# A decoder layer on Trainium2: keys, queries and two value blocks of its memory attention as paired products

## The chip, the cores and the metric

The kernel runs on one core of one Trainium2 chip. The metric is the device time of one execution in microseconds. Before the change it is 1982.21 us, the median of three runs (1981.88 to 1982.49). One execution was also recorded with a hardware profiler; that execution took 1980.76 us, and its span from first to last instruction is 1979.0 us.

A core has five engines, each with its own queue of instructions that it works through in the order of the program: TensorE does matrix products (PE in the profile, and PEld for its loads of the stationary operand), VectorE (DVE) and ScalarE (ACT) do elementwise work, GpSimd (POOL) does a few small operations here, and SyncE (SP) issues the DMA transfers.

## The reference, cut to what matters

One layer with four stages, of which the third is the one that changes. `x` is 256 tokens by 2048, `mem` is 256 memory tokens by 2048, and there are 4 heads of 512.

```python
def rmsnorm(x, w):
    y = x * lax.rsqrt(jnp.mean(x * x, axis=-1, keepdims=True) + 1e-6)
    return y * w

def memory_cross_attention(hn, mem_n, w_q, w_k, w_v, w_o):
    q = (hn @ w_q).reshape(b, s, 4, 512)
    k = (mem_n @ w_k).reshape(b, m, 4, 512)
    v = (mem_n @ w_v).reshape(b, m, 4, 512)
    logits = jnp.einsum("bshd,bmhd->bhsm", q, k) * 512 ** -0.5
    p = jax.nn.softmax(logits, axis=-1)
    o = jnp.einsum("bhsm,bmhd->bshd", p, v).reshape(b, s, 2048)
    return o @ w_o

def layer(x, mem, ...):
    ...                                     # retention and RG-LRU mixers, gated merge
    h = x + merged @ w_mix_out
    h = h + memory_cross_attention(rmsnorm(h, norm_xa_w), rmsnorm(mem, norm_mem_w), ...)
    h = h + conv_gated_ffn(rmsnorm(h, norm_ffn_w), ...)
    return rmsnorm(h, final_norm_w)
```

All of it is float32.

## The kernel before, in words

**Products.** A float32 product is made of three products of float32r parts. Every operand is split into a rounded part `hi` and a rest `lo`, and hi*hi, lo*hi and hi*lo are added up in PSUM (`products_n`, lines 404 to 411). One product of a 128x128 stationary block with a 128x512 moving block is thus three matmuls. All matmuls are kept in the order in which the program text asks for them.

**Weights.** The weights lie in one DRAM array in the order of use, and are loaded by SP in chunks of 1 MB into three buffers `raw`. `prefetch` (line 273) keeps the split parts of the next chunks ready (`AHEAD = 2`): `weight_parts` (line 344) makes `hi` with a cast on ACT (line 349) and `lo` with a subtraction on DVE (line 350), each into one of six buffers (`PART_BUFS = 6`). A buffer comes free when the matmuls of the chunk that lies in it are done. Each chunk is one step of a counter; `later(n, fn)` (line 377) runs `fn` some steps on.

**Single products.** `gemm_n`/`steps_n` (line 413) makes one block of 512 output columns for 256 tokens in four steps of 24 matmuls. Its left side is a list of eight split tiles, each for two of the sixteen 128-row blocks of the contraction. Where that list is made on demand (class `Pairs`, line 661: `xs` for x, `ms` for the memory tokens), the single product asks for tiles ahead of their use, in line 434: `st[min(NT, k0 + 3 * n) // 2 - 1]`.

**Pairs.** `pair`/`steps_pair` (line 475) makes two blocks of 512 columns at once in eight steps. An ordinary step has 24 matmuls. In the steps named by a tuple (`SEVEN = (2, 5)` and others) the 2x2 blocks of tokens and columns are multiplied with seven products in place of eight, so 21 matmuls. Such a step needs sums of weight blocks (`seven_parts`, line 364: four additions on DVE, line 370, and 3.5 casts and subtractions of 128x1024) and sums of token blocks (`sums_of`, line 442: a sum of the parts, three differences, a rounding on ACT in line 458 and a rest on DVE in line 459). A pair uses all eight PSUM banks: three tiles of `acc` and the two tiles of `sm` (`small`, line 209). After its last step the banks are added up into two row tiles `o` (lines 511 to 530). The lines on the left side of a pair are

```python
for i in seven:
    if k2 < i <= k2 + 3 and (not isinstance(st, list) or i < len(st)):
        sums_of(st[i])
t = st[k2]
```

so sums are made up to three steps ahead for tiles that exist, and `st[k2]`, asked for in the step that uses it, makes the tile if it does not exist yet.

**Turning.** `by_dma` (line 544) turns rows into columns: ACT copies the rows into planes of 16-bit halves (line 552), SP issues two transposing DMAs, and some steps later ACT joins the halves (line 565).

**Memory attention.** The residual rows `hrow` (four tiles of 256 tokens by 512 columns) get the product with `w_mix_out` added (`residual`, line 1008; the addition is line 1023) and are turned into `h1s`, eight split tiles. Meanwhile `memory_steps` (line 1045) makes the row norms of the memory tokens and the first four of the eight tiles of `ms`. Then, for each of the four heads, `key_query` makes the keys (`xa_w_k` with `ms`) and the queries (`xa_w_q` with `h1s`) as single products; `softmax` (line 1065) follows a few steps later, with the logits in one of the two `sm` tiles. Four single products for the values follow, each with `attend` (line 1109), and then the output product with `xa_w_o`, whose first two blocks are already a pair. `hrow` stays in SBUF all the time. The pool `big` has 29 buffers of 4 KB per partition, and nearly everything named here lies in it.

Of the kernel before, what the change touches and what calls it, by code (L numbers as in the profile page):

```python
# [9 lines left out]
F32 = mybir.dt.float32  # L10
# [7 lines left out]
P = 128  # L18
D = 2048
S = 256  # L20
NT = D // P
# [3 lines left out]
XH = 4  # L25
XD = D // XH
FF = 5632
# [47 lines left out]
def weight_plan():  # L75
# [12 lines left out]
    plan += [("w_mix_out", 0, NT, b * BW) for b in range(4)]  # L88
    plan += [(w, 0, NT, b * BW) for b in range(4) for w in ("xa_w_k", "xa_w_q")]
    plan += [("xa_w_v", 0, NT, b * BW) for b in range(4)]  # L90
    plan += [both("xa_w_o", 0, SEVEN_O)] + [("xa_w_o", 0, NT, b * BW) for b in (2, 3)]
# [74 lines left out]
def hybrid_layer(  # L166
# [23 lines left out]
    sp_ = ctx.enter_context(tc.tile_pool(name="sp", bufs=2))  # L190
    pm = ctx.enter_context(tc.tile_pool(name="pm", bufs=3, space=bass.MemoryType.PSUM))
    px = ctx.enter_context(tc.tile_pool(name="px", bufs=2, space=bass.MemoryType.PSUM))

# [243 lines left out]
    def gemm_n(*args):  # L437
        return ended(steps_n(*args))
# [35 lines left out]

    def steps_pair(w, row, st, nk, c1, c2, seven=SEVEN):

        last = max(seven)
        banks, begun = {}, set()
# [53 lines left out]
    def pair(*args):  # L532
        return ended(steps_pair(*args))
# [279 lines left out]
    for g in range(2):  # L813
# [18 lines left out]
        if g == 1:  # L832
            vs += [split_rows(v, rs0) for v in pair("w_in", 0, xs, NT, O_V + 1024, O_V + 1024 + BW, SEVEN_V)]
        qr, kr = turned
# [173 lines left out]
    def residual(w, st, out, wcol, steps=None):  # L1008

        ss = sums()  # L1010
        products = [steps_n(w, 0, st, NT, b * BW) for b in range(4)]
        sources = []
        for b in range(4):
            if steps:
                steps(b)
                if b == 0:
                    for one in products[:3]:
                        for _ in range(2):
                            next(one)
            elif b == 0:  # L1020
                sources += pair(w, 0, st, NT, 0, BW, SEVEN_O)
            h = hrow[b]
            dve.tensor_add(h, h, sources.pop(0) if sources else ended(products[b]))
            by_dma(h, lambda f, b=b: turn(f, b, out, wcol), 1 + (b == 1), b == 3 and steps is None)
            if b < 2:
                later(2 + b, lambda h=h, b=b: squares(h, ss, b))
            else:
                squares(h, ss, b)
        return ss
# [25 lines left out]

    h1s = []
    ss1 = residual("w_mix_out", merged, h1s, p_xa, memory_steps)


    lscale = sp_.tile([P, 2], F32, tag="ls", name="lscale")  # L1060
# [29 lines left out]
    def split_block(f, out, seven=()):  # L1090
        for pr in range(2):
            with_sums(out, seven, f[:, 2 * pr : 2 * pr + 2, :])
        return out

    def key_query(b):
        ks = []
        turned_rows(gemm_n("xa_w_k", 0, ms, NT, b * BW), rsms[0], lambda f: split_block(f, ks))

        def query(f):
            qs = split_block(f, [])  # L1100
            later(1, lambda: softmax(b, qs, ks))

        turned_rows(gemm_n("xa_w_q", 0, h1s, NT, b * BW), None, query)

    for b in range(XH):
        key_query(b)
    osp = []
# [13 lines left out]

    for b in range(XH):
        v = split_rows(gemm_n("xa_w_v", 0, ms, NT, b * BW), rsms[0])
        later(1, lambda b=b, v=v: attend(b, v))

    h2s = []
# [113 lines left out]
    def up(b, hid, seven):  # L1240
# [6 lines left out]

        two = pair("ffn_w_up", 0, h2s, NT, b * BW, FF + b * BW, SEVEN_U)
        for a, then, wait in zip(two, (lambda f: conv(f, 4 * b, gt), value), (1, 3)):
# [61 lines left out]
```

## Time and profile before

| | before |
|---|---|
| median of 3 runs | 1982.21 us |
| the profiled execution: its time | 1980.76 us |
| the profiled execution: its span | 1979.0 us |
| TensorE matmul, share of the span | 99% |
| VectorE, ScalarE, share of the span | 79%, 69% |
| DMA, mean rate | 215 GB/s |

How to read the profile lines below: the page has a line of busy times for each engine, and a chain of waits that is followed back from the last instruction. A group line reads `line engine operation output<-inputs shapes xcount | busy us, mean ns of one | idle time before, and what ended it`. A timeline line reads `start us, us, engine line operation xcount [idle before <-what ended it]`. A line of a view of stretches has, for each engine, its busy time and the number of its instructions, then the granted TensorE clock, the share of the DMA engines and their rate. A line of waits has the engine and tile that waited, for whom, us in total, how often, and the longest.

### The profile page before, as it was taken

The numbers are of one execution on the slowest core, as the hardware profiler recorded it, in microseconds if no ns is written. First come the engines' busy times: TensorE is split into PE (matmuls) and PEld (weight loads), VectorE is DVE, ScalarE is ACT, GpSimd is POOL, SyncE is SP. The second block draws the span as 40 slices with busy tenths as digits, with TensorE's granted clock in tenths as the row PEclk, the third lists the DMA queues.
The fourth block names the chain that finished last, engine by engine and source line by source line (L and its number), as shares of the span: only waits on it lengthen the run. The fifth ranks groups of instructions, "written<-read, shape, count | busy, mean of one in ns | idle before, by whom it ended". The sixth has DMA issues, their size and how long they took to land.

```text
span 1979.0 us, 24013 instructions
## 1 busy us (share of the span) xinstructions
PE 1965.8 (99%) x8834; PEld 1631.4 (82%) x8834; DVE 1564.5 (79%) x2050; ACT 1367.1 (69%) x1671; POOL 26.8 (1%) x25
## 2 busy tenths in 40 slices
PE   9999999999999999999999999999999999999998
PEld 7888788888888888888888888888888888888887
DVE  6887986899898888767555567778889878898686
ACT  7666657989654656697676667777776578774683
POOL 0000010010000000000000000000000000000000
PEclk9999999999999999999999999999999999999999
DMA  9755567666555465887676657666666566666673
GB/s 334 238 213 173 194 232 203 213 210 212 194 212 189 176 228 192 297 277 226 218 222 206 203 170 223 210 216 213 224 207 208 212 211 215 215 210 233 214 252 110
DMA packets 197190, 425.62 MB, mean 215 GB/s; under 512 B 142032, under 2 KB 146640, under 8 KB 152016
## 3 DMA queue, kind: packets, MB, share of 16 engines
q1 hardware_dynamic: 197072, 424.09, 64.2%
q8 instruction: 69, 1.13, 0.2%
q14 instruction: 49, 0.40, 0.1%
HBM read 388.39 MB, written 2.10 MB: 197 GB/s over the span
## 4 chain that ended last, share of the span: by engine, by line
PE 91%; DVE 3%; ACT 3%; issue 1%; DMA 1%; SPq 0%; POOL 0%; POOLq 0%; DVEq 0%; ACTq 0%
PE acc L251 66%; PE sm L251 25%; DVE lo L350 1%; DMA raw<-in_wall 1%; ACT hi L349 1%; ACT f L565 1%; ACT pl L552 0%; DMA pt<-pl 0%; DVE xr L932 0%; DVE tb L734 0%; ACT rows L804 0%; DMA raw<-in_head 0%; DVE fv L1138 0%; DVE o L530 0%; DVE raw L370 0%
## 5 line engine op out<-in xcount | busy, mean ns | idle before, releaser
L251 PE MATMUL acc<-hi,s 128*128 128x512 f32 (+1 forms) x3976 | 1218.7, 388 | 0.2 <-ACT s L611 0.2
L350 DVE TENSOR_TENSOR lo<-raw,hi 128x1024 fp32r<-128x1024 f32 (+1 forms) x794 | 931.8, 1197 | 325.7 <-ACT hi L349 315.8
L349 ACT CAST hi<-raw 128x1024 fp32r<-128x1024 f32 (+1 forms) x794 | 788.3, 1023 | 401.1 <-PE acc L251 126.6
L251 PEld LDWEIGHTS acc<-hi,s 128*128 128x128 f32 x3976 | 743.4, 188 | 152.4 <-ACT s L611 0.5
L251 PE MATMUL acc<-lo,s 128*128 128x512 f32 (+1 forms) x1988 | 771.0, 388 | 1.4 <-DVE lo L350 1.4
L251 PEld LDWEIGHTS acc<-lo,s 128*128 128x128 f32 x1988 | 373.3, 188 | 79.8 <-DVE lo L350 3.1
L251 PE MATMUL sm<-hi,s 128*128 128x512 f32 x1344 | 414.0, 389 | 1.6 <-DVE o L530 1.6
L251 PEld LDWEIGHTS sm<-hi,s 128*128 128x128 f32 x1344 | 252.1, 188 | 55.0 <-ACT v L600 1.8
L251 PE MATMUL sm<-lo,s 128*128 128x512 f32 x672 | 261.5, 389 | 0.0
L565 ACT COPY f<-pt 128x1024 uint16<-128x1024 uint16 x128 | 167.1, 1353 | 36.2 <-DMA pt<-pl 35.8
L251 PEld LDWEIGHTS sm<-lo,s 128*128 128x128 f32 x672 | 126.2, 188 | 26.1
L370 DVE TENSOR_TENSOR raw<-raw 128x512 f32<-128x512 f32 x160 | 110.0, 687 | 2.4
L251 PE MATMUL acc<-hi,ts 128*128 128x512 f32 x240 | 73.9, 389 | 0.0
L552 ACT COPY pl<-rows 128x1024 uint16<-128x1024 uint16 x56 | 55.7, 1042 | 24.8 <-DVE rows L576 13.3
L552 ACT COPY pl<-o 128x1024 uint16<-128x1024 uint16 x52 | 51.6, 1038 | 6.7 <-DVE o L1000 6.7
L251 PEld LDWEIGHTS acc<-hi,ts 128*128 128x128 f32 x240 | 45.0, 188 | 9.3
L251 PE MATMUL acc<-lo,ts 128*128 128x512 f32 x120 | 47.1, 393 | 1.4 <-DVE lo L350 1.3
L1138 DVE SCALAR_TENSOR_TENSOR fv<-f,pf,fv 128x255 f32<-128x255 f32 (+1 forms) x88 | 38.3, 476 | 0.0
L530 DVE TENSOR_TENSOR o<-o,acc 128x512 f32<-128x512 f32 x52 | 33.2, 678 | 5.7 <-PE acc L251 5.7
L1138 DVE SCALAR_TENSOR_TENSOR fg<-f,pf,fg 128x255 f32<-128x255 f32 (+1 forms) x88 | 35.8, 477 | 0.0
L520 DVE TENSOR_TENSOR o<-o,acc 128x512 f32<-128x512 f32 x52 | 35.2, 678 | 0.0
L530 DVE TENSOR_TENSOR o<-o,sm 128x512 f32<-128x512 f32 x52 | 33.9, 677 | 0.1
(190 smaller groups left out, 1010.8 us busy)
## 6 DMA issues: line engine op xcount, KB each, us to landing
raw<-in_wall SPq DMA_DIRECT2D x352, 1024.0 KB, 4.9
nat<-in_x SPq DMA_DIRECT2D x8, 512.0 KB, 9.2
raw<-in_wall SPq DMA_DIRECT2D x7, 512.0 KB, 6.2
pt<-pl SPq DMA_TRANSPOSE x128, 3.3
nat<-in_mem SPq DMA_DIRECT2D x4, 512.0 KB, 8.9
xt<-in_x_t SPq DMA_DIRECT2D x3, 512.0 KB, 9.3
xt<-in_mem_t SPq DMA_DIRECT2D x3, 512.0 KB, 6.4
dec<-in_consts SPq DMA_DIRECT2D x2, 512.0 KB, 4.4
```

The lines of the kernel that those rows point to most:

```text
L251: tc.keep_in_program_order(pe.matmul(*a, **k))
L349: act.copy(hi[:, cs], src[:, cs])
L350: dve.tensor_tensor(out=lo[:, cs], in0=src[:, cs], in1=hi[:, cs].bitcast(F32), op=ALU.subtract)
L370: dve.tensor_tensor(out=o, in0=a, in1=b, op=ALU.add)
L520: dve.tensor_tensor(out=o, in0=a, in1=b, op=op)
L530: dve.tensor_tensor(out=o, in0=o, in1=banks[a], op=ALU.add)
L552: act.copy(planes[:, tt], words[:, tt])
L565: act.copy(halves_[:, :, :, cs], turned_[:, :, :, cs])
L1138: dve.scalar_tensor_tensor(out=y[:, s:S], in0=z[:, j, 0 : S - s], scalar=pf[:, 2 - s, t : t + 1], in1=y[:, s:S], op0=ALU.mult, op1=ALU.add,)
```

## The change

Keys, queries and the first two value blocks become pairs with seven products in steps 2 and 5: keys of heads 0 and 1, queries of 0 and 1, queries of 2 and 3, then the softmax of heads 0 and 1, keys of 2 and 3, values of 0 and 1, the softmax of heads 2 and 3, and the values of 2 and 3 as single products as before. The key rows are scaled in place on ACT and turned directly, where before DVE scaled or copied each block's rows out of PSUM. The stored token sums are dropped after the first pair of keys, and made again for the second. The four residual tiles are stored to DRAM when they are complete, and loaded again before the output product. A pair takes its tuple of seven-product steps from the plan of the weights rather than from its caller, with the same values as before for the old pairs.

```diff
--- before.py
+++ after.py
@@ -86,8 +86,8 @@
     plan += [both("w_in", O_GB + 1024), both("w_proj_rnn", 1024)]
     plan += [both(w, c + b * BW) for w, c in (("w_in", O_GA), ("w_proj_ret", 0)) for b in (0, 2)]
     plan += [("w_mix_out", 0, NT, b * BW) for b in range(4)]
-    plan += [(w, 0, NT, b * BW) for b in range(4) for w in ("xa_w_k", "xa_w_q")]
-    plan += [("xa_w_v", 0, NT, b * BW) for b in range(4)]
+    plan += [both(w, b * BW) for w, b in (("xa_w_k", 0), ("xa_w_q", 0), ("xa_w_q", 2), ("xa_w_k", 2))]
+    plan += [both("xa_w_v", 0)] + [("xa_w_v", 0, NT, b * BW) for b in (2, 3)]
     plan += [both("xa_w_o", 0, SEVEN_O)] + [("xa_w_o", 0, NT, b * BW) for b in (2, 3)]
     for kind, *a in ff_plan():
         if kind == "down" and sum(a) < NF // 4:
@@ -189,6 +189,7 @@
     tp = ctx.enter_context(tc.tile_pool(name="tp", bufs=10))
     sp_ = ctx.enter_context(tc.tile_pool(name="sp", bufs=2))
     pm = ctx.enter_context(tc.tile_pool(name="pm", bufs=3, space=bass.MemoryType.PSUM))
+    home = ctx.enter_context(tc.tile_pool(name="home", bufs=4, space=bass.MemoryType.DRAM))
     px = ctx.enter_context(tc.tile_pool(name="px", bufs=2, space=bass.MemoryType.PSUM))
 
     count = [0]
@@ -472,8 +473,9 @@
             sums_of(t, src, scale)
         out.append(t)
 
-    def steps_pair(w, row, st, nk, c1, c2, seven=SEVEN):
-
+    def steps_pair(w, row, st, nk, c1, c2):
+
+        seven = plan[gemms[0]][3][2]
         last = max(seven)
         banks, begun = {}, set()
         banks["p2"], banks["p4"] = (lambda a: (a[:, 0, :], a[:, 1, :]))(acc())
@@ -830,7 +832,7 @@
                 v = gemm_n("w_in", 0, xs, NT, O_V + b * BW) if b else ended(v_steps)
                 vs.append(split_rows(v, rs0))
         if g == 1:
-            vs += [split_rows(v, rs0) for v in pair("w_in", 0, xs, NT, O_V + 1024, O_V + 1024 + BW, SEVEN_V)]
+            vs += [split_rows(v, rs0) for v in pair("w_in", 0, xs, NT, O_V + 1024, O_V + 1024 + BW)]
         qr, kr = turned
         gates = []
         c = O_G + g * 1024
@@ -1018,7 +1020,7 @@
                         for _ in range(2):
                             next(one)
             elif b == 0:
-                sources += pair(w, 0, st, NT, 0, BW, SEVEN_O)
+                sources += pair(w, 0, st, NT, 0, BW)
             h = hrow[b]
             dve.tensor_add(h, h, sources.pop(0) if sources else ended(products[b]))
             by_dma(h, lambda f, b=b: turn(f, b, out, wcol), 1 + (b == 1), b == 3 and steps is None)
@@ -1053,9 +1055,18 @@
             for k2 in range(4):
                 later(2 + k2, lambda k2=k2: ms[k2])
 
-    h1s = []
+    h1s, parked = [], []
+
+    def park(h):
+        t = home.tile([P, 2, BW], F32, tag="home", name=nm("home"))
+        sp.dma_start(out=t, in_=h)
+        parked.append(t)
+
     ss1 = residual("w_mix_out", merged, h1s, p_xa, memory_steps)
 
+
+    for h in hrow:
+        park(h)
 
     lscale = sp_.tile([P, 2], F32, tag="ls", name="lscale")
     dve.tensor_scalar_mul(lscale, rstd_rows(ss1), float(XD**-0.5))
@@ -1092,18 +1103,22 @@
             with_sums(out, seven, f[:, 2 * pr : 2 * pr + 2, :])
         return out
 
-    def key_query(b):
-        ks = []
-        turned_rows(gemm_n("xa_w_k", 0, ms, NT, b * BW), rsms[0], lambda f: split_block(f, ks))
-
-        def query(f):
-            qs = split_block(f, [])
-            later(1, lambda: softmax(b, qs, ks))
-
-        turned_rows(gemm_n("xa_w_q", 0, h1s, NT, b * BW), None, query)
-
-    for b in range(XH):
-        key_query(b)
+    keys, queries = {}, {}
+
+    def turned_pair(w, st, b, r, out):
+
+        for i, a in enumerate(pair(w, 0, st, NT, b * BW, (b + 1) * BW)):
+            if r is not None:
+                with tc.high_priority(FREE):
+                    for tt in range(2):
+                        act.mul(a[:, tt, :], a[:, tt, :], r[:, tt : tt + 1])
+            o = out[b + i] = []
+            by_dma(a, lambda f, o=o: split_block(f, o), 1 + i)
+
+    def attention(b):
+        for i in (b, b + 1):
+            softmax(i, queries[i], keys[i])
+
     osp = []
 
     def attend(b, v):
@@ -1119,9 +1134,24 @@
                 )
         turned_rows(a, None, lambda f: split_block(f, osp, SEVEN_O))
 
-    for b in range(XH):
+    turned_pair("xa_w_k", ms, 0, rsms[0], keys)
+    token_sums.clear()
+    turned_pair("xa_w_q", h1s, 0, None, queries)
+    turned_pair("xa_w_q", h1s, 2, None, queries)
+    attention(0)
+    turned_pair("xa_w_k", ms, 2, rsms[0], keys)
+    for b, a in enumerate(pair("xa_w_v", 0, ms, NT, 0, BW)):
+        v = split_rows(a, rsms[0])
+        later(b, lambda b=b, v=v: attend(b, v))
+    attention(2)
+    for b in (2, 3):
         v = split_rows(gemm_n("xa_w_v", 0, ms, NT, b * BW), rsms[0])
         later(1, lambda b=b, v=v: attend(b, v))
+
+    for b in range(4):
+        t = big([P, 2, BW], s="nat")
+        sp.dma_start(out=t, in_=parked[b])
+        hrow[b] = t
 
     h2s = []
     ss2 = residual("xa_w_o", osp, h2s, p_ffn)
@@ -1245,7 +1275,7 @@
             conv(f, NF + 4 * b, vl)
             gate_up(gt, vl, hid, seven)
 
-        two = pair("ffn_w_up", 0, h2s, NT, b * BW, FF + b * BW, SEVEN_U)
+        two = pair("ffn_w_up", 0, h2s, NT, b * BW, FF + b * BW)
         for a, then, wait in zip(two, (lambda f: conv(f, 4 * b, gt), value), (1, 3)):
             with tc.high_priority(FREE):
                 for tt in range(2):
```

## What the change should do to the time

> **What bounds the kernel now.** I read the page first: busy times, then the chain that ended last.
>
> ```profile
> span 1979.0 us, 24013 instructions
> ...
> PE 1965.8 (99%) x8834; PEld 1631.4 (82%) x8834; DVE 1564.5 (79%) x2050; ACT 1367.1 (69%) x1671; POOL 26.8 (1%) x25
> ...
> PE 91%; DVE 3%; ACT 3%; issue 1%; DMA 1%; SPq 0%; POOL 0%; POOLq 0%; DVEq 0%; ACTq 0%
> ```
>
> TensorE sets the end. Next the chain in order of time, through the stage that changes (stretch 885 to 1180):
>
> ```profile
> 958.95 2.87 PE sm L251 x24
> 961.82 43.55 PE acc L251 x192
> 1005.37 2.87 PE sm L251 x24
> ...
> 1101.08 76.19 PE acc L251 x336
> ```
>
> It is matmuls only. The softmax logits (24 matmuls on `sm`, 2.87 us) interrupt the projections (192 in 43.55 us, so 0.2268 us each) without a hole. So every matmul removed here is worth its 0.2268 us, and every wait added on TensorE costs its full length; DVE and ACT count only where they are late.
>
> How close are they to late? The stretches view sets an old pair stage beside the first key and query blocks:
>
> ```profile
> 516.00:559.00 43.00, 43.00 (x191) 35.62 (x190) 39.60 (x52) 21.95 (x25) 0.00 (x0) 1.00 0.52 196
> 893.70:959.00 65.30, 65.30 (x290) 54.08 (x289) 41.92 (x51) 46.31 (x59) 0.70 (x1) 1.00 0.79 240
> ```
>
> In the old pairs DVE is busy 39.60 of 43 us and TensorE still never idles. In the stage to be changed DVE has 23 us to spare in 65.
>
> **What is removed.** Five pairs replace ten single products; each has two steps of 21 matmuls in place of 24, so 5 x 2 x 3 = 30 matmuls go: 30 x 0.2268 = **-6.80 us**. Nothing else leaves TensorE.
>
> **What is added to DVE and ACT on average.** The prices:
>
> ```profile
> L350 DVE TENSOR_TENSOR lo<-raw,hi 128x1024 fp32r<-128x1024 f32 x98 | 117.7, 1221 | 98.3 <-ACT hi L349 92.7 <-PE acc L251 4.0
> L349 ACT CAST hi<-raw 128x1024 fp32r<-128x1024 f32 x98 | 100.7, 1048 | 39.9 <-PE acc L251 34.2 <-issue 3.5 <-ACT pl L552 1.6
> L454 DVE TENSOR_TENSOR tq<-f 128x256 f32<-128x256 f32 x2 | 0.9, 426 | 0.1
> L459 DVE TENSOR_TENSOR ts<-tq,ts 128x512 fp32r<-128x512 f32 x1 | 0.7, 685 | 0.0
> L458 ACT CAST ts<-tq 128x512 fp32r<-128x512 f32 x1 | 0.6, 622 | 0.0
> L455 DVE TENSOR_TENSOR tq<-tq,f 128x128 f32<-128x128 f32 x2 | 0.6, 292 | 0.1
> L456 DVE TENSOR_TENSOR tq<-f,tq 128x128 f32<-128x128 f32 x1 | 0.3, 285 | 0.0
> L612 DVE SCALAR_TENSOR_TENSOR s<-xt,pb,s 128x256 fp32r<-128x256 f32 x8 | 3.5, 485 | 0.0
> L611 ACT ACTIVATE s<-xt,pb 128x256 fp32r<-128x256 f32 x8 | 3.4, 495 | 0.0
> L370 DVE TENSOR_TENSOR raw<-raw 128x512 f32<-128x512 f32 x160 | 110.0, 687 | 2.4
> L350 DVE TENSOR_TENSOR lo<-raw,hi 128x512 fp32r<-128x512 f32 x46 | 31.1, 684 | 2.6 <-ACT hi L349 2.6
> L448 DVE TENSOR_TENSOR g<-s 128x512 f32<-128x512 f32 x9 | 6.1, 682 | 0.0
> L520 DVE TENSOR_TENSOR o<-o,acc 128x512 f32<-128x512 f32 x52 | 35.2, 678 | 0.0
> ```
>
> A seven-product step adds four additions (2.75) and 1.5 subtractions (1.9) on DVE; ten of them make 47 us, six token sums of 2.4 another 14. Over some 280 us that leaves DVE near the share of the old pairs. On average this costs nothing; the cover is the spare DVE time above.
>
> **Where it is late: the first pair of keys.** A single product asks for tiles of `ms` ahead; a pair doesn't. `memory_steps` makes tiles 0 to 3. Tiles 4 to 7, and the sums of tile 5, are then asked for in the very step that uses them, and in the changed program's order of instructions they stand behind the weight splits of a later step. Those wait for TensorE, as ScalarE's timeline in an old pair shows:
>
> ```profile
> 752.93 1.05 ACT L349 CAST hi<-raw 128x1024 fp32r<-128x1024 f32 x1
> 755.58 1.05 ACT L349 CAST hi<-raw 128x1024 fp32r<-128x1024 f32 x1 [1.60 <-PE acc L251]
> 758.30 1.05 ACT L349 CAST hi<-raw 128x1024 fp32r<-128x1024 f32 x1 [1.67 <-PE sm L251]
> 761.02 1.05 ACT L349 CAST hi<-raw 128x1024 fp32r<-128x1024 f32 x1 [1.67 <-PE acc L251]
> ```
>
> The casts come 2.72 us apart, one per 12 matmuls: each waits until TensorE frees the buffer six tiles back. A cast that stands ahead of something the *running* step needs thus makes TensorE wait for itself plus a chain. Step by step, in us from the step's start (0.1 to 0.2 per hand-over from TensorE):
>
> *Step 5.* Its second product takes the token sums. In order: the second cast of step 6 on ACT (its buffer is freed only when step 4 ends), its subtraction on DVE, two differences, the rounding on ACT, the rest on DVE: 0.2 + 1.05 + 1.22 + 0.29 + 0.29 + 0.62 = 3.67 for the first matmul, + 0.69 = 4.36 for the second, which was due after four matmuls at 0.91. **Wait 3.5.** Bounds: 3.0 (only the first) to 3.9 (DVE later than its inputs).
>
> *Step 6.* Tile 6 is rounded on ACT behind both casts of the next pair's first chunk; the second takes the buffer freed at step 5's end, at 0.45 with a bank copy ahead of it. DVE then does the subtraction, one bank sum, the rest of the tile's first half, two bank sums, and the rest of the second half: 1.5 + 0.3 (DVE still in the chunk before) + 1.22 + 0.68 + 0.49 = 4.0 less overlaps of 0.1, then 1.36 + 0.49 = 5.6. The second half's rest was due at 0.91. **Wait 4.7.** Bounds 4.2 to 5.5.
>
> *Step 2.* Its sums are asked for in time, but DVE is behind. Up to the addition of the last residual block the instruction order of both programs agrees, so before's DVE timeline dates it:
>
> ```profile
> 893.38 3.48 DVE L350 TENSOR_TENSOR lo<-raw,hi 128x1024 fp32r<-128x1024 f32 x3
> 896.79 1.21 DVE L1023 TENSOR_TENSOR nat<-nat,acc 128x1024 f32<-128x1024 f32 x1
> ...
> 902.47 0.17 DVE L1061 TENSOR_SCALAR lscale<-ro 128x2 f32<-128x2 f32 x1 [0.26 <-POOL ro L657]
> ```
>
> Three instructions in 3.48 are 1.13 apart, so they overlap by 0.08. From 898.0: a half subtraction, four additions and the sum of the parts (3.7), the first differences and small ones (0.75), the wait for POOL's root ahead of `lscale` (to 903.35), two subtractions, the last difference, one more subtraction, the rest of the sums: 907.7. The key product starts 288 matmuls before 958.95, at 893.63; the matmul was due 52 later, at 905.4. **Wait 2.3**, bounds 0 to 3.
>
> *Step 4* would start at 917.0. ACT reaches tile 4 only behind joins of the last residual block and four casts:
>
> ```profile
> L565 ACT COPY f<-pt 128x1024 uint16<-128x1024 uint16 x128 | 167.1, 1353 | 36.2 <-DMA pt<-pl 35.8
> ```
>
> From 906.6: two joins, two casts, four roundings of 0.41, two and a half casts, then the tile: 916.2. DVE's rests follow between weight additions at 917.95 and 919.0, due at 917.2 and 918.7. **Wait 1.1**, bounds 0 to 2. Step 7's tile comes with tile 6, ahead of need: 0.
>
> After that TensorE's lateness helps the next pair: its step 2 sums are ready at about 956 against a need at 958. The second key pair finds all tiles made: 0.
>
> **Softmax between pairs.** The logits take the `sm` bank of the pair that just ended, and TensorE waits for the bank's addition. Before, such waits were short:
>
> ```profile
> PE acc L251 <- DVE lo L350: 2.6, 5, 0.8
> PE sm L251 <- DVE o L530: 1.6, 2, 1.4
> ```
>
> In the new DVE order one subtraction, whose cast waits for the last step's first half, stands ahead of that addition: 0.4 us past the end, twice. **0.8**, bounds 0 and 2 x 1.4. The two banks must then be free for the next pair, which wants them 8.9 and 10.2 us after the end.
>
> ```profile
> L1074 DVE TENSOR_REDUCE sx<-sm 128x2 f32<-128x512 f32 x4 | 2.8, 692 | 3.2 <-PE sm L251 3.2
> L1081 ACT ACTIVATE prob<-sm,sx,lscale 128x256 f32<-128x256 f32 x8 | 4.5, 560 | 12.1 <-DVE sx L1075 12.1
> ```
>
> The first logits end at 3.3; their maximum (0.69, behind weight additions), the scale and two exponentials of 0.75 with the read of their sums end at 6.5. The second head's maximum stands behind the first's reciprocal in DVE's order: to 7.3, and its exponentials to 9.6. 0.6 us of cover; if that goes, TensorE waits for what is missing: 0, bound 1 for the two.
>
> **Parking.** Four stores and four loads on SP's queue:
>
> ```profile
> raw<-in_wall SPq DMA_DIRECT2D x352, 1024.0 KB, 4.9
> nat<-in_x SPq DMA_DIRECT2D x8, 512.0 KB, 9.2
> ```
>
> Each store waits for its block's addition; behind it stand that block's transposes, which wait for a copy of the same result anyway, then weights for a step that is two or more ahead. The loads stand between the chunks for steps 4 and 5 of the output product and wait for buffers that the last value product frees; step 5's weights, five steps of 5.44 us away, land in 4.9, and the rows (9.2) are wanted after a 43 us pair. 0; without that cover, one landing, 4.9 to 9.2. Their eight issues fall into times in which SP waits for buffers anyway.
>
> Scaling the key rows moves from DVE to ACT, four operations of a pair as in
>
> ```profile
> L1252 ACT ACTIVATE o<-o,ro 128x512 f32<-128x512 f32 x44 | 29.6, 715 | 3.4 <-DVE o L530 3.4
> ```
>
> 2.9 us, with the plane copies ahead of the second cast of the query pair's step 2; that cast ends some 5 us before its step by the same tally: 0, and what exceeds 5 us if that cover goes. Making the memory sums again is in the 14 us above. POOL gets nothing new.
>
> **Sum.** -6.80 + 2.3 + 1.1 + 3.5 + 4.7 + 0.8 = **+5.6 us**. The profiled execution's own 1980.76 becomes 1986.4; it lay 1.45 under the median, so I forecast 1982.2 + 5.6 = **1987.8 us**. All low bounds give -6.8 + 7.2 = +0.4 (1982.6), all high ones -6.8 + 18.2 = +11.4 (1993.6).
>
> **Rivals.**
>
> *The saving stays whole: 1975.4 us.* For it: the old pairs hide as much DVE work at TensorE idle 0. Against: there all left tiles existed. It decides whether ACT gets to tiles 5 and 6 before steps 5 and 6 begin; with six buffers the cast in front can't. 13%.
>
> *Only the two structural waits remain, partly: about 1981 to 1985*, so no change that shows. For it: the DVE backlog in steps 2 and 4 is a tally of many small terms. 12%.
>
> *The clock falls in the waits: 1992.7 us.* In the last stretch, after the final matmuls:
>
> ```profile
> 1972.00:1979.00 7.00, 0.00 (x0) 0.00 (x0) 2.04 (x7) 1.12 (x2) 0.54 (x1) 0.65 0.39 151
> ```
>
> an idle TensorE shows a mean clock of 0.65, a loss of 0.35 x 7 = 2.45 us. If the waits in steps 5 and 6 each bring that, +4.9. Against: their longest single holes are 3.0 and 1.8 us, with matmuls between. 8%. [...]
>
> *Weights late behind the parked rows: 1992 or more*, by one landing, if a reload's buffer is freed only after the output product has begun. 5%.
>
> **How the numbers follow.** The forecast has 62%. 0.2% (4 us) is about what a measurement of this kernel can tell from no change: 1978.2 to 1986.2. Of the forecast's 62%, 12 points fall under 1986.2 and count as same with the second rival's 12: same 0.25. Faster 0.13, slower 0.62. The range has to reach below the summed low bounds towards the first rival, and above to the clock: 1980 to 1994.
>
> **What would show it.** In the first key pair, TensorE waiting for `ts` (step 5) and for `s` of line 612's helper (step 6), some 3.5 and 4.7 us, both new in the view of waits, and smaller ones in steps 2 and 4; 30 fewer matmuls; no other hole over 1 us up to the output product. No waits on `ts` and `s`, or a clock under 1.00 in that stretch, would prove me wrong.

## The result, and the profile after

| | before | after |
|---|---|---|
| median, four runs each, same chip | 1982.05 us | **1992.28 us** (1991.34 to 1992.62) |
| ratio | | 1.0052, 95% interval 1.0038 to 1.0067 |
| the profiled execution: time, span | 1980.76, 1979.0 us | 1992.14, 1990.0 us |
| mean granted clock | 0.999 | 0.996 |

Slower by 10.2 us; 5.6 had been forecast, and the range held it. The busy times on the page after:

```profile
span 1990.0 us, 24148 instructions
PE 1966.6 (99%) x8804; PEld 1628.2 (82%) x8804; DVE 1632.3 (82%) x2164; ACT 1392.4 (70%) x1710; POOL 26.1 (1%) x25
```

TensorE has its 30 matmuls less (8834 to 8804) and yet is busy 0.8 us longer: some of what is left runs more slowly. To see where, I measure one **stage** in every run: from the first matmul of the first key product to the first of the output product. TensorE's timeline of after has both starts:

```profile
893.11 0.61 PE L252 MATMUL acc<-hi,s 128*128 128x512 f32 x2
...
1185.01 0.62 PE L252 MATMUL acc<-hi,s 128*128 128x512 f32 x2
```

That is 291.9 us; before it is 280.9 (893.51 to 1174.39). Outside this stage the two agree: the first key product starts within 0.4 us of the same time, the last addition behind the output product begins 89.2 us after that product's start in both, and from that start to the end of the span the two differ by 0.4 us. So the whole loss, 11.0 us of span, lies in the stage. TensorE's waits there (before has none in these stretches):

```profile
PE sm L252 <- ACT ts L459: 3.8, 2, 3.2
PE acc L252 <- DVE s L614: 2.2, 2, 1.7
PE acc L252 <- ACT s L613: 1.4, 1, 1.4
PE sm L252 <- DVE o L532: 1.4, 2, 1.0
PE sm L252 <- DVE ts L460: 0.8, 2, 0.6
PE acc L252 <- DVE ps L1127: 0.3, 1, 0.3
```

The waits on `ts` (token sums) and on `s` (tiles of `ms`) are the forecast ones. Two others stand beside them: `o`, the bank additions ahead of the two softmaxes, and `ps`, the attention's probabilities. In order of time, TensorE's timeline in steps 5 and 6 of the first key pair (its waiting rows alone):

```profile
926.24 0.51 PE L252 MATMUL sm<-hi,ts 128*128 128x512 f32 x1 [3.25 <-ACT ts L459]
926.96 0.79 PE L252 MATMUL sm<-hi,ts 128*128 128x512 f32 x1 [0.22 <-DVE ts L460]
934.00 0.51 PE L252 MATMUL acc<-hi,s 128*128 128x512 f32 x1 [1.41 <-ACT s L613]
936.15 0.50 PE L252 MATMUL acc<-hi,s 128*128 128x512 f32 x1 [1.65 <-DVE s L614]
937.74 0.80 PE L252 MATMUL acc<-hi,s 128*128 128x512 f32 x1 [0.58 <-DVE s L614]
```

The second column is telling: the matmuls at 926.96 and 937.74 take 0.79 and 0.80 us, the others 0.50 to 0.51. The view of stretches shows why (the columns are busy time and count of PE, PEld, DVE, ACT and POOL, then the granted clock, which is TensorE's clock as a share of full speed):

```profile
925.00:930.00 5.00, 3.54 (x8) 2.65 (x9) 2.28 (x5) 2.54 (x3) 0.00 (x0) 0.67 0.79 277
930.00:935.00 5.00, 3.09 (x12) 1.90 (x11) 4.22 (x5) 4.12 (x8) 0.00 (x0) 0.99 0.47 157
935.00:940.00 5.00, 3.26 (x8) 2.31 (x9) 3.48 (x8) 0.14 (x1) 0.00 (x0) 0.69 0.71 262
940.00:945.00 5.00, 5.00 (x16) 3.92 (x15) 1.23 (x1) 1.05 (x1) 0.00 (x0) 0.62 0.01 3
```

The clock fell twice. From 940 to 945 TensorE never waits, and does 16 matmuls where 22 fit. By their starts, the matmuls behind each fall come 0.427 us apart in place of 0.227, 7 of them from 926.96 on and 14 from 937.74 on; this costs 1.40 + 2.75 = 4.15 us.

Why the sums were late at 926: ScalarE's timeline, then VectorE's.

```profile
922.17 1.05 ACT L350 CAST hi<-raw 128x1024 fp32r<-128x1024 f32 x1 [1.07 <-PE sm L252]
925.57 0.62 ACT L459 CAST ts<-tq 128x512 fp32r<-128x512 f32 x1 [2.34 <-DVE tq L457]
```

```profile
923.79 1.22 DVE L351 TENSOR_TENSOR lo<-raw,hi 128x1024 fp32r<-128x1024 f32 x1
924.92 0.28 DVE L456 TENSOR_TENSOR tq<-tq,g 128x128 f32<-128x128 f32 x1
925.24 0.29 DVE L457 TENSOR_TENSOR tq<-g,tq 128x128 f32<-128x128 f32 x1
926.21 0.69 DVE L460 TENSOR_TENSOR ts<-tq,ts 128x512 fp32r<-128x512 f32 x1 [0.68 <-ACT ts L459]
```

It is the chain that the prediction wrote out: a cast of the *next* step's weights waits for TensorE, VectorE does its subtraction at 923.79 ahead of two short differences, and only then are the sums rounded. VectorE took the subtraction up 0.57 us after its cast had ended, as it was still at the sum of the parts.

### The profile page after: what moved, and what is told of

It reads as the page before. It is cut to its first block, busy times and chain, and to the rows that moved or that the text cites. A ratio compares the mean times of both kernels' runs of the same rounds, so it can differ in the third digit from the quotient of the medians.

```text
span 1990.0 us, 24148 instructions
## 1 busy us (share of the span) xinstructions
PE 1966.6 (99%) x8804; PEld 1628.2 (82%) x8804; DVE 1632.3 (82%) x2164; ACT 1392.4 (70%) x1710; POOL 26.1 (1%) x25
## 4 chain that ended last, share of the span: by engine, by line
PE 37%; DVE 8%; ACT 4%; DMA 2%; issue 2%; POOL 0%; POOLq 0%; DVEq 0%; ACTq 0%; SPq 0%
PE acc L252 23%; PE sm L252 14%; DVE lo L351 3%; ACT hi L350 1%; DMA raw<-in_wall 1%; DMA pt<-pl 1%; ACT f L567 1%; ACT pl L554 1%; DVE fg L1168 1%; DVE raw L371 1%; DVE fv L1168 1%; DVE o L522 1%; ACT o L1282 0%; DVE s L591 0%; DVE fo L1179 0%
## 5 line engine op out<-in xcount | busy, mean ns | idle before, releaser
L252 PE MATMUL acc<-hi,s 128*128 128x512 f32 (+1 forms) x3636 | 1116.8, 389 | 3.9 <-DVE s L614 2.2
L252 PEld LDWEIGHTS acc<-hi,s 128*128 128x128 f32 x3636 | 680.8, 188 | 145.0 <-DVE s L614 4.3
L252 PE MATMUL acc<-lo,s 128*128 128x512 f32 (+1 forms) x1818 | 705.8, 388 | 2.0 <-DVE lo L351 1.9
L252 PE MATMUL sm<-hi,s 128*128 128x512 f32 x1584 | 488.7, 390 | 1.9 <-DVE o L532 1.9
L252 PEld LDWEIGHTS acc<-lo,s 128*128 128x128 f32 x1818 | 341.9, 188 | 73.4 <-DVE lo L351 3.2
L252 PEld LDWEIGHTS sm<-hi,s 128*128 128x128 f32 x1584 | 297.8, 188 | 64.7 <-ACT v L602 2.0
L252 PE MATMUL sm<-lo,s 128*128 128x512 f32 x792 | 308.5, 390 | 0.0
L252 PEld LDWEIGHTS sm<-lo,s 128*128 128x128 f32 x792 | 148.9, 188 | 31.0
L371 DVE TENSOR_TENSOR raw<-raw 128x512 f32<-128x512 f32 x200 | 138.1, 691 | 3.1
L522 DVE TENSOR_TENSOR o<-acc,o 128x512 f32<-128x512 f32 x62 | 40.0, 690 | 0.4
```

Of the source, the lines that this page charges most:

```text
L252: tc.keep_in_program_order(pe.matmul(*a, **k))
L371: dve.tensor_tensor(out=o, in0=a, in1=b, op=ALU.add)
L522: dve.tensor_tensor(out=o, in0=a, in1=b, op=op)
```

## The experiments

Twelve kernels ran. Stage times are from one profiled execution each, run times are medians beside the kernel before on the same chip:

| run | us | before, same chip | ratio, 95% interval | stage |
|---|---|---|---|---|
| before | 1982.05 | | | 280.9 |
| after | 1992.28 | 1982.05 | 1.0038 to 1.0067 | 291.9 |
| e1_ahead | 1983.14 | 1982.73 | 0.9993 to 1.0012 | 283.8 |
| e2_single | 1983.14 | 1982.73 | 0.9999 to 1.0017 | 280.8 |
| e3_park | 1983.81 | 1982.73 | 0.9995 to 1.0013 | 281.5 |
| e4_warm | 1990.33 | 1982.73 | 1.0025 to 1.0055 | 287.8 |
| e5_late | 1990.74 | 1982.47 | 1.0027 to 1.0053 | 291.5 |
| e7_early | 1984.01 | 1982.47 | 0.9997 to 1.0016 | 283.6 |
| e8_ahead2 | 1984.60 | 1982.47 | 0.9997 to 1.0015 | 283.4 |
| e9_sums | 1986.10 | 1982.47 | 1.0003 to 1.0023 | 283.9 |
| e11_scale | 1981.91 | 1982.89 | 0.9983 to 1.0001 | 279.6 |
| e12_acc | 1992.07 | 1982.89 | 1.0033 to 1.0057 | 290.4 |
| e13_pool | 2002.21 | 1982.89 | 1.0084 to 1.0114 | 299.9 |
| e17_seven | 1992.60 | 1982.30 | 1.0030 to 1.0064 | 289.8 |

Single executions of the kernel before lay between 1979.4 and 1987.8 us, so a few us are read from the stage rather than from medians. A stage is one execution too. Between executions of programs with the same instruction order up to there, step 2 of the first key pair alone lost 1.7 to 5.6 us, and the second softmax 0.9 to 4.0 over the runs that keep its logits on `sm`; where it matters, the text therefore names the step and not only the sum.

**The clock by itself.** Zeros are multiplied into the open bank where TensorE waited (32 matmuls; they add 0):

```diff
+        fill = {(0, 40): 14, (1, 40): 2, (0, 46): 6, (1, 46): 7, (1, 47): 3} if w == "xa_w_k" and c1 == 0 else {}
...
+                for _ in range(fill.get((i, filled[0]), 0)):
+                    mm(o, zeros, right[0], start=False, stop=False, skip_group_check=True)
```

> The changed kernel with 32 added matmuls of zeros (they add 0 to the open bank) in the five longest waits of the first key pair, so that TensorE works through them: 14 and 2 before the two halves of step 5's sums, 6, 7 and 3 in step 6. The waits themselves stay. Theory (the clock halves because TensorE idles there, and that costs 1.8 in step 5 and 2.9 in step 6): the granted clock stays at 1.00 from 925 to 945 and the time falls by 4.7 less what the zeros overrun (up to 1), to 1987.6 to 1988.6. Rival (the clock's fall is only how the records show a waiting TensorE, and costs nothing of its own): the time stays at 1992.3 or rises by the overrun.

The stage fell by 4.1 us. Its stretches:

```profile
925.00:930.00 5.00, 4.95 (x22) 3.63 (x21) 2.57 (x5) 2.62 (x3) 0.00 (x0) 1.00 0.86 311
...
940.00:945.00 5.00, 5.00 (x23) 4.13 (x22) 2.91 (x3) 1.74 (x2) 0.00 (x0) 1.00 0.07 10
```

The clock stays at 1.00, TensorE does 23 matmuls where it did 16, and the gain equals the 4.15 worked out above. The clock's fall is a cost of its own, on top of the waits: the rival is out. The median fell less, by about 2.6 relative to before, and missed the theory's band for the time. The profiled execution lost 1.8 to after in the feed-forward stage, which lasted 680.6 to 685.1 us over these runs; that this is also what the medians lost is not shown.

**Everything three steps ahead.**

```diff
             k2 = k0 // KH
+            if isinstance(st, Pairs):
+                st[min(NT // 2, k2 + 4) - 1]
             for i in seven:
```

> One line is added to steps_pair: before step k's token sums are made, the tile of the memory that lies three steps ahead is made too, so that the first key pair has its tiles 4 to 7, and the sums of tile 5, before the casts of later weights are queued. Theory (the tiles and sums made just in time are the cause, and the clock falls only because of their waits): in the changed kernel steps 4, 5 and 6 of the first key pair last 0.7 + 7.1 + 5.8 = 13.6 us longer than their matmuls need; all but at most 1 of it goes, the granted clock stays at 1.00 there, step 2's 1.8 stays, and the time is 1992.3 - 12.6 to 13.6 = 1978.7 to 1979.7, below the kernel before. Rival (DVE and ACT have too much to do in the first pair, whatever the order): the waits move to steps 2 to 4 and sum to 6 or more there, time 1985 or above.

The loss of steps 4 to 6, 13.6 us, went entirely, but the stage fell by only 8.1. TensorE's waits in the stage:

```profile
PE sm L252 <- ACT ts L459: 2.8, 1, 2.8
PE sm L252 <- DVE o L534: 1.3, 2, 0.9
PE sm L252 <- DVE ts L460: 1.2, 2, 0.7
PE acc L252 <- DVE lo L351: 0.6, 1, 0.6
```

Step 2 waited for its sums so long that the clock fell (5.6 in all, 1.8 in after), and the query pair, without a wait in after, now lost 1.8. Neither forecast of the time held: the median, 1983.14, lies between the theory's 1978.7 to 1979.7 and the rival's 1985, and steps 2 to 4 lost 5.6, the clock included, where the rival has 6 or more of waits.

**Which of the two late tiles.** Only tiles 6 and 7 ahead (`if k2 == 5: st[7]`), then only tiles 4 and 5 with their sums (`if k2 == 2: st[5]`):

> The changed kernel; only tiles 6 and 7 of the memory are made ahead, in step 5 of the first key pair, before that step's own sums are asked for. Stage times (from the first matmul of the first key pair to that of the output product) are 280.88 before and 291.91 as changed. Theory (steps 5 and 6 each wait for their own late tile, and each wait brings its own fall of the clock): step 6's 5.8 go and step 5's 7.1 stay or grow by up to 1, stage 286.1 to 287.1, run about 6 above before. Rival (one late chain behind both): with step 5 still late, step 6 still waits 2 or more, stage 288.5 or more.

> The changed kernel; only tiles 4 and 5 and the sums of tile 5 are made ahead, in step 2 of the first key pair; tiles 6 and 7 stay just in time. Theory: step 5's 7.1 go with its fall of the clock, and step 4's 0.7; step 6's 5.8 stay, stage 284.1 to 285, run about 4 above before. Rival (the lateness only moves on): step 6 or the first query pair waits for what step 5 no longer waits for, stage 288 or more.

Each edit removed its own step's loss. With tiles 6 and 7 ahead, step 6 lost 0 and step 5 kept 7.4; the stage missed the theory's figure all the same, because step 2 lost 5.2 in that execution (in after 1.8) and the second softmax 3.5 (1.1). With tiles 4 and 5 ahead, step 5 kept 0.9 of 7.1, step 6 lost 3.9 of 5.8, and the stage came out 0.5 below its forecast. So the two waits are separate. Step 6 lost less than the 5.8 that were to stay: its wait was 1.6 us in place of 2.2, and the other 1.3 us are put down to the clock, an estimate (mean over the execution 0.999, in after 0.996).

**Ahead from step 2 only.** The line of the second experiment with `and k2 >= 2`.

> As in the first of these experiments, but the tiles are made three steps ahead only from step 2 on; there, tile 3 had been pulled in front of the addition of the last residual block, which then came 3.2 us later, and step 2 waited 5.5 with a fall of the clock in place of 1.8. Theory: steps 4, 5 and 6 lose their 13.6, step 2 keeps 1.8 with the clock at 1.00, the query pair, which is now wanted earlier, waits up to 2.7 for its sums: stage 278.3 to 281.0 (before: 280.88), run 3 below before to level with it. Rival (DVE is behind whatever the order): step 2 or the query pair wait 4 or more, stage 282 or above.

One reason given there is wrong. In e1_ahead's program the orders of VectorE and ScalarE up to the last residual block's addition are those of after: no tile was pulled in front. The addition varies by execution. It began 2.6 us after the first key product in after and 4.8 to 4.9 in e1_ahead and e5_late, where ScalarE waited for transposed rows several times; with it, step 2's loss ran from 1.7 to 5.6 us. The theory's stage missed too, and the rival's figures came: the stage was 283.4. Step 2 lost 1.8 and steps 4 to 6 lost 0.4, but the first query pair lost 4.9, of which 3.3 are waits and the rest the clock. The rival's reason, VectorE behind whatever the order, is not what the trace shows. The pair's waiting rows, then ScalarE's and VectorE's timelines ahead of them:

```profile
952.07 0.50 PE L252 MATMUL sm<-hi,ts 128*128 128x512 f32 x1 [2.14 <-ACT ts L459]
953.15 0.51 PE L252 MATMUL sm<-hi,ts 128*128 128x512 f32 x1 [0.58 <-DVE ts L460]
```

```profile
938.43 1.33 ACT L1116 ACTIVATE o<-o,ro 128x512 f32<-128x512 f32 x2
939.66 1.98 ACT L556 COPY pl<-o 128x1024 uint16<-128x1024 uint16 x2
941.55 1.34 ACT L1116 ACTIVATE o<-o,ro 128x512 f32<-128x512 f32 x2
942.79 1.98 ACT L556 COPY pl<-o 128x1024 uint16<-128x1024 uint16 x2
944.67 1.57 ACT L350 CAST hi<-raw 128x512 fp32r<-128x512 f32 x2
```

```profile
945.32 0.69 DVE L351 TENSOR_TENSOR lo<-raw,hi 128x512 fp32r<-128x512 f32 x1 [2.17 <-ACT hi L350]
```

ScalarE scales and copies both key blocks (938.43 to 944.67) before it turns to the cast that VectorE needs; VectorE stands idle 2.17 us and then has the query pair's sums behind that. In after this was covered: TensorE came to the query pair 13 us later.

**The key rows later.** On top of the last edit, the scaling and plane copies of a pair's key blocks are asked for in steps 3 and 6 of the next pair:

```diff
-            if r is not None:
-                with tc.high_priority(FREE):
-                    for tt in range(2):
-                        act.mul(a[:, tt, :], a[:, tt, :], r[:, tt : tt + 1])
+            def scaled(a=a, o=o):
+                for tt in range(2):
+                    act.mul(a[:, tt, :], a[:, tt, :], r[:, tt : tt + 1])
+                by_dma(a, lambda f: split_block(f, o))
+            later(2 + 3 * i, scaled)
```

> As the run that makes tiles three steps ahead from step 2 on (stage 283.42; there the first query pair waited 3.3 for the sums of its step 2 and the clock fell: 4.9 in all). In that run DVE stood idle 2.17 us for a cast that ScalarE had put behind the scaling and the plane copies of both key blocks (6.4 us). Here the first key block of a pair is scaled and copied two steps later, the second five steps later. Theory (that queue is what makes the query pair's sums late): its wait falls under 1.2, no fall of the clock, stage 279.2 to 280.0. Rival (DVE has too much to do, ScalarE's queue was not it): wait 2 or more, stage 282 or above.

In the trace only the plane copies moved there (958.12 and 974.39); the four scalings still ran at the head of the query pair (941.74 to 944.83), with a cast between them. So about 4 of the 6.4 us left the queue ahead of the casts. The stage is 279.6, inside the theory's band. The query pair loses nothing, the clock stays at 1.00, and these waits are left:

```profile
PE sm L252 <- DVE o L534: 2.0, 2, 1.2
PE sm L252 <- ACT ts L459: 0.8, 1, 0.8
PE sm L252 <- DVE ts L460: 0.6, 1, 0.6
PE acc L252 <- DVE ps L1134: 0.2, 1, 0.2
```

The run is 10 us faster than after, and 1 us below before, which its interval does not tell from no change.

**Step 2's sums earlier.** As e8_ahead2, with `later(6, lambda: sums_of(ms[2]))` in `memory_steps`.

> As the run before it, with the sums of the memory's tile 2 made during the third block of the residual, ahead of the last block's addition. Theory (step 2's sums are late only for their place in DVE's order): step 2's 1.8 go as well and the stage is 1.8 shorter than in the run before it, or as much less as the query pair then waits for its own sums. Rival: the four operations (2.4 us) only push back the last block's addition, and step 2 or the query pair wait as long as before: stage as in the run before it, within 0.5.

The rival's stage held (283.9 against 283.4), but not by its means. Step 2 lost 0 in place of 1.8 and the last block's addition was not pushed back (2.0 us after the first key product, 2.6 in the run before); step 5 lost 3.7 and the query pair 3.8. That VectorE's 2.4 us of work came back there as a wait is likely, not shown.

**The logits on an `acc` bank.** As e11_scale, with `two = acc()` for both heads in place of two `small()`.

> As the run before, with the logits of both heads on an acc bank instead of two sm banks. Theory (TensorE waits ahead of the softmax for the additions on the sm banks alone, 0.55 and 0.9 to 1.1): both waits go, stage 1.4 to 1.6 shorter than in the run before. Rival (the acc bank that comes next in turn is the one that the pair's first two additions free): no gain, or up to 1 longer where the next pair's step 2 then waits for a bank that an exponential still reads.

Neither. The wait for the additions went, but a longer one came, in the middle of the logits (TensorE's timeline, second softmax):

```profile
1126.61 3.78 PE L252 MATMUL acc<-s,s 128*128 128x256 f32 x16 [5.39 <-ACT prob L1093]
```

With both heads in one tile, the second head's logits waited, here 5.39 us, until the first head's exponentials had read theirs. The stage grew by 10.8. Whether two separate tiles would have gained was not tried.

**Sums on GpSimd.** As e12_acc, with the additions and differences of `sums_of` issued on GpSimd for these pairs.

> As the run before, with the additions and differences of the token sums of this attention's pairs on GpSimd (1.7 us of DVE time a sum go there; rounding and rest stay). Theory (step 2 of the first key pair waits 1.8 because its sums stand in DVE's queue): this wait and what is left in the query pair go, stage 1.5 to 2.5 shorter than in the run before. Rival (GpSimd is too slow for them, or takes DVE's time by sharing its way to memory): a sum takes over 5 us there, steps 2 wait 2 or more longer, stage above the run before.

Step 2's loss did fall, from 1.7 to 0.7, but step 5's rose from 0.4 to 8.2. GpSimd's timeline there, then VectorE's additions over the first two pairs, in this run and in e11_scale:

```profile
923.21 1.27 POOL L450 TENSOR_TENSOR g<-s 128x512 f32<-128x512 f32 x1
```

```profile
L371 DVE TENSOR_TENSOR raw<-raw 128x512 f32<-128x512 f32 x16 | 12.3, 770 | 0.3
```

```profile
L371 DVE TENSOR_TENSOR raw<-raw 128x512 f32<-128x512 f32 x16 | 11.0, 687 | 0.2
```

GpSimd took 1.27 us or more where VectorE took 0.68, and VectorE's own additions lasted 12% longer on average over the two pairs (770 ns against 687). The rival's stage held, by other waits than it named: step 2 did not grow. In step 5 TensorE waited 3.53 us for the rest of the weights (`lo`), not for the token sums; VectorE's additions on the weights took 0.94 to 1.22 us there while GpSimd worked.

**One more split buffer.** `PART_BUFS = 7`, general buffers 28, small ones 9. An earlier form (e16_seven), which took two general buffers and no small one, deadlocks and has no time; the gain of 10 us expected of it is the first rival below.

> The changed kernel with seven buffers for the split weights in place of six, paid for with one of the 29 general buffers and one of ten small ones; no tile is made earlier. In the program's order of instructions the sums of tile 5 then stand behind one cast more than before, and seven back of that cast is the same buffer as six back of the last one before; tile 6 stands behind the same casts as before. Theory (what delays a tile is the cast ahead of it, which waits for TensorE to free its buffer): step 5 keeps its 7.1 within 1; in step 6 the cast ahead takes a buffer that comes free one earlier, at most 2.7, so of its 5.8 between 2 and 5 are left: stage 288 to 291.1 (291.91 as changed). First rival (one more buffer brings each cast 2.72 forward whatever the order): steps 5 and 6 lose 2.7 each and both falls of the clock, stage 282. Second rival (buffers have no part in it, the tiles are late for the work ahead of them): stage 291.9 within 0.7, both steps as they were. Two other buffers fewer may cost elsewhere, so the stage decides and not the run's time.

The stage was 289.8. Step 5 lost 8.7 (its rows include step 6's first wait, as the 7.1 did), step 6 0.8. The theory held for the stage, partly by luck: step 5 grew by 1.6, not at most 1, step 6 fell further than to its 2, and the second softmax, of which the theory says nothing, added 1.8. The second rival is out, as step 6 did change. The first rival is out: the added buffer went into one more cast ahead of the sums, and step 5 waits longer than in after:

```profile
929.16 1.52 PE L252 MATMUL sm<-hi,ts 128*128 128x512 f32 x2 [4.42 <-ACT ts L459]
```

**Singles for the first keys.** Two single products in place of the first key pair; the rest as changed.

> The first key pair is two single products again; queries, the second key pair, the value pair, softmax and parking stay as changed. 24 fewer matmuls than before. Theory (all of the loss but some 2.2 us lies in the first key pair): 1982.05 - 24 x 0.2268 + 1.65 (banks held by softmax) + 0.55 (attention's wait) = 1978.8 us, clock 1.00 up to the output product. Rival (another pair, the parking or the longer softmax costs as well and was only covered by the first pair's holes): 1982 or more, with new holes over 1 us behind the first query pair.

The two key products lost 0.1 and the query pairs nothing, so the first key pair's loss is its own. But the stage was 280.8, not the theory's 277.6, and the rival's figures came (1983.14, and a hole over 1 us). The second softmax waited 2.25 for its bank (1.0 in after), and the clock fell (TensorE's timeline, then two stretches):

```profile
1115.61 5.58 PE L253 MATMUL sm<-s,s 128*128 128x256 f32 x32 [2.25 <-DVE o L533]
```

```profile
1113.19:1116.60 3.41, 1.16 (x9) 0.99 (x9) 3.41 (x6) 3.28 (x5) 0.00 (x0) 1.00 0.83 291
1116.60:1120.01 3.41, 3.41 (x18) 3.41 (x18) 2.21 (x4) 0.33 (x1) 0.00 (x0) 0.50 0.04 17
```

**Parking alone.** The kernel before with the four stores and four loads.

> The kernel before with the parking alone: the four residual blocks are stored to DRAM after the first residual and read back before the output product; no pair is added. Theory: no cost, 1982.05 within 1 us, no new wait of TensorE on a DMA. Rival (the four stores and loads delay weights on their queue, or the rows return late): one landing, 4.9 to 9.2 us more, so 1987 to 1991.

The theory held in kind. TensorE waits for no DMA, and the stage is 0.6 longer through one wait on a tile. The median is 1.1 us above before on the same chip, just over the theory's 1, but its interval does not tell that from no change. The transfers in its list of DMA issues (KB each, us to landing):

```profile
home<-nat SPq DMA_DIRECT2D x4, 512.0 KB, 6.8
nat<-home SPq DMA_DIRECT2D x4, 512.0 KB, 6.9
```

Each lands in about 7 us, and none of that shows in the run's time: the rival's 4.9 us or more is outside the interval, which ends at 2.6. What stays open is 0.7 us outside the span (2.5 us there, 1.8 before).

## Why the prediction was right in direction and half in size

| term of the sum | forecast | in after |
|---|---|---|
| 30 matmuls | -6.8 | -6.8 |
| step 2 | 2.3 (0 to 3) | 1.8 |
| step 4 | 1.1 (0 to 2) | 0.7 |
| step 5 | 3.5 (3.0 to 3.9) | 3.9 |
| step 6 | 4.7 (4.2 to 5.5) | 4.4 |
| softmax between pairs | 0.8 (0 to 2.8) | 1.65 |
| attention's wait on `ps` | not in the sum | 0.55 |
| the clock | 0; rival of 8% at 2 x 2.45 | 4.15 |

**The mechanism of the waits was right.** The four waits of the first key pair sum to 10.8 (11.6 forecast), each inside its bounds, step 5 at the upper end, with steps 5 and 6 held by the operations that were named. Making the tiles ahead removed those of steps 4 to 6 (e1_ahead, e8_ahead2), steps 5 and 6 each separately (e5_late, e7_early). The allowance of 0.1 to 0.2 per hand-over from TensorE was too large, at no cost to the sum: the cast at 922.17 follows the start of step 5's first matmul, 922.14, by 0.03.

**The step that failed was the clock**, left out of the sum because "their longest single holes are 3.0 and 1.8 us, with matmuls between". The holes came out near the forecast (3.25 and 1.65), and the clock fell all the same. What the prediction named as a sign of its being wrong, a clock under 1.00 in that stretch, came true. e4_warm shows that this is worth 4.1 us. The longest single hole was the wrong measure: ahead of the two falls TensorE idled 2.96 and 2.14 us in all within 3.41 us (last section). The rival had the mechanism, but its price agrees by luck: 2.45 a fall is the mean over 7 us in which the clock stood at 1.00 up to 1974.09 and at 0.50 from there, and the falls cost 1.40 and 2.75. After's trace also shows the return, 1.00 again from 930.10 and from 943.75, so the clock stood at 0.50 for 3.41 us the first time and for 6.83 the second.

**Softmax** was forecast at half its size, inside its bounds; it also varies much (0.5 to 4.0 us at one softmax over the runs that keep the logits on `sm`). **`ps`** was missed: the rounded probabilities of head 2 stand behind weight splits on VectorE, so the attention product waits.

**Cover.** The price of scaling the key rows on ACT, "0, and what exceeds 5 us if that cover goes", held in after. But its cover was the lateness of the first pair: in e8_ahead2, without that lateness, scaling and copies cost the query pair up to 4.9. The same holds for "TensorE's lateness helps the next pair". "On average this costs nothing" holds for the pairs in the middle of the stage (excess 0 in queries 2 and 3 and in keys 2 and 3 apart from the softmax), not for the first 84 us: in e9_sums work moved ahead there removed one wait and left others of the same length. **Parking** at 0 held for the transfers (e3_park).

Not accounted for: the rows of the table add up to 10.35 us, and the stage grew by 11.0, so 0.65 us of it stands in no row. Another 0.4 us lies outside the span (2.14 us after, 1.76 before); the two profiled executions differ by 11.4, the medians by 10.2.

## What to carry to other kernels

When an order of instructions is fixed, ask for each operand made just in time what stands ahead of it on its engine, and make it before the casts of later weights are queued: one line was worth 8 us here. When such a wait goes, price the next pair again without the cover that the wait gave; here one ScalarE queue took 4.9 us of the gain, and moving it gave 3.8 of them back. When you forecast several short waits close together, add up TensorE's idle time over them rather than look at the longest hole (in after 2.96 and 2.14 us within 3.41 us stood ahead of the two falls), and put the likely cost of the clock, here 1.40 and 2.75 us, into the sum, not into a rival.

## What the runs showed of the hardware

**In after, the clock changed at places 3.41 and 6.83 us apart, behind stretches in which TensorE had idled 2.96 and 2.14 us.** When the stretches of the view are narrowed around a fall, the granted clock reads 1.00 or 0.50 and nothing between. In this stage it changes at 926.68, 930.10, 936.92 and 943.75. In slices of 3.41 us that end at these places, after reads (the first column after the length is TensorE's busy time; the rest of the slice it was idle):

```profile
923.27:926.68 3.41, 0.45 (x1) 0.19 (x1) 2.66 (x6) 0.62 (x1) 0.00 (x0) 1.00 0.97 320
926.68:930.10 3.42, 3.20 (x8) 2.48 (x8) 1.41 (x2) 2.02 (x2) 0.00 (x0) 0.50 0.63 264
...
933.51:936.92 3.41, 1.27 (x4) 0.67 (x4) 3.41 (x6) 1.63 (x5) 0.00 (x0) 1.00 0.82 296
936.92:940.34 3.42, 2.83 (x7) 2.12 (x7) 1.56 (x4) 0.00 (x0) 0.00 (x0) 0.50 0.65 275
940.34:943.75 3.41, 3.41 (x9) 2.64 (x9) 1.23 (x1) 1.05 (x1) 0.00 (x0) 0.50 0.02 5
```

The 2.14 us ahead of the second fall are the wait of 1.65 and the last 0.49 of the one of 1.41. The clock fell once more at the end of after (1984.81) and once at the end of before (1974.09), behind slices with 1.99 and 2.34 us idle. With slices of the same length laid through both traces from these places, the idlest at full clock that was followed by full clock had 1.66 us (after, from 230.36). These are four falls in two executions, and no run varied the idle time alone; e4_warm, with the holes filled, kept 1.00. The second fall of after cost twice the first as its first slow slice, with 0.58 us idle, was followed by another at 0.50, where that of the first fall, with 0.22 idle, was followed by 1.00; that the hole of 0.58 decided this is not shown.

A longer wait did not always cost more. e2_single waited 2.25 us (above), within one slice, and the next slice read 0.50. e17_seven waited 2.78 us at the same place, and the clock stayed at 1.00. Counted in steps of 3.413 us from near 934.0, where its matmuls go back from 0.427 to 0.227 us apart, a slice ends at 1125.13 and cuts that wait into 1.28 and 1.50 us idle:

```profile
1121.72:1125.13 3.41, 2.13 (x10) 1.44 (x8) 3.41 (x5) 1.79 (x3) 0.00 (x0) 1.00 0.45 137
1125.13:1128.55 3.42, 1.92 (x16) 1.92 (x17) 3.42 (x6) 2.76 (x4) 0.00 (x0) 1.00 0.85 290
```

That this kept the clock up is not shown: no run moved the wait alone. The two waits lie differently in their slices: e2_single's begins 0.17 us into one, e17_seven's 2.13. Nothing on record before these runs gave that place, so a forecast could only give such a fall odds and a likely cost.

**The start of e11_scale's execution was slower than before's.** Between 4 and 10 us it has 14 matmuls in 5.58 us of busy time, where before has 23 in 5.79. The first key product began at 896.8 in place of 893.5. Whether such a start is part of why single executions of one kernel differ by up to 8 us is not shown.

**VectorE was slower while GpSimd worked beside it.** In e13_pool its additions on the weights took up to 1.22 us in place of 0.68 during GpSimd's sums, 12% more on average over the two pairs. GpSimd itself took 1.27 to 3.40 us for an addition that took VectorE 0.68; how long it takes alone was not measured.
